# Down weights in 8 KB runs and gate_up in four sections: one MoE kernel on one core

## The chip, the cores and the metric

One Trainium2 chip; the kernel runs on one of its cores. The metric is the device time of one execution in microseconds (us). The engines are named as the profile names them: PE is TensorE (PEld its weight loads), DVE VectorE, ACT ScalarE, POOL GpSimd, SP SyncE, which issues the transfers. A "q" behind an engine's name is its sequencer, which waits, branches and issues.

## The reference

One encoder layer on 256 tokens of width 1024: three token mixers, a merge, a LayerNorm, then a mixture of experts with 32 experts of which each token takes four. The change touches the experts alone:

```python
def expert_block(args):
    xe, e = args
    h = xe @ w_gu[e] + b_gu[e]
    gate, up = h[:, :D_FF], h[:, D_FF:]
    gate = jnp.minimum(gate, SWIGLU_LIMIT)
    up = jnp.clip(up, -SWIGLU_LIMIT, SWIGLU_LIMIT)
    return ((up + 1) * (gate * jax.nn.sigmoid(SWIGLU_ALPHA * gate))) @ w_dn[e] + b_dn[e]
...
x = _layernorm(DN_ALPHA * x + ffn, ln2_g[l], ln2_b[l])
```

Each expert has a gate_up matrix of 1024 x 2048 and a down matrix of 1024 x 1024 in float32, 12 MB together. An expert's output rows are weighted by the token's gate and added to the token's row.

## The kernel before

The mixers take the first 390 us. Behind them a loop runs over the 32 experts.

**Weights.** An expert's weights are twelve tiles of 128 x 2048 float32 (1 MB): u = 0 to 7 are gate_up, u = 8 to 11 are down. `load` (L743 to L753) issues one transfer per tile on SP, in this order, into a ring of 19 slots; the transfer that takes a slot over waits until PE has done with the tile in it. The first 19 tiles are loaded during the mixers, in halves, by `do_pre`. In `wgu_v` a partition's row of a gate_up tile is one run of 8 KB in HBM. In `wdn_v` a down tile holds 256 rows of the matrix: partition p gets row p and row 128 + p of it, two runs of 4 KB.

**Tokens.** An expert's count of tokens is known only at run time. `size` is 0 for up to 32 tokens, 1 for 33 to 64, 2 for more. `expert` loads it into the engines' registers (L1198) and chooses by `tc.If`: `up_many` and the block under `both > 0` work on 64 tokens, `up_four` and the block under `both != 1` on 32. So an expert runs "four" alone, "many" alone, or both. More than 96 (`TOP`) go through the loop `heavy` (L1341), which stands in front of the last expert under an If of its own, "overflow" (L1419); with these inputs it isn't run.

**One expert on PE.** PE's order is the order of the code (`pe_order`). Gate_up runs in two sections of four tiles, `for k0 in (0, KT // 2)` (L1250): `up_many` under one If (L1251), `up_four` under the next (L1253). A bias matmul opens each accumulation (L1233 for many, L1243 for four), L1237 and L1247 are the products. Between the sections stand

- `flush(prev)`: the previous expert's rows `yh` and `yl` (a high and a low part) are scattered by matmuls with `sc` (L1172) into PSUM tiles `pos`, two for tokens 0 to 127 (c = 0), two for tokens 128 to 255 (c = 1), and DVE adds them to the sum `acc` (L1176). `pos` has two buffers, so c = 1 waits for the adds of c = 0;
- `aux`: one matmul with `rankT` (L1258) and 24 of a single column (L1119), from which slots and gates are read.

Then DVE and ACT make the gated product `uv` (tokens on partitions, 256 columns), PE turns it by two transposes per tile (L1280 for many, L1303 for four), each of 128 neighbouring columns, ACT copies the result to `hT`, and the down products follow (L1287, L1318). `weigh` makes `yh` and `yl`, which the next expert's flush takes up. In front of the overflow loop the last flush ran by itself, since that loop used the same `sc`, `yh` and `yl`.

The other engines' order is set by the framework's scheduler.

Of the kernel before, what the change touches and what calls it, by code (L numbers as in the profile page):

```python
# [10 lines left out]
F32R = mybir.dt.float32r  # L11
# [170 lines left out]
def tile_trunk(ctx, tc, xT_d, xn_d, wf_d, vec_d, row_d, rw_d, cst_d, cst2_d, rope_d, ln1_d, ln2_d,  # L182
# [539 lines left out]
    wdn_v = wdn_d.rearrange("e (h u k p) n -> e u h p k n", h=2, u=2, p=P)  # L722
# [9 lines left out]
    def do_pre(n):  # L732
        e, u = divmod(n, 12)
        assert n == nload[0]
        t = ring_tile(f"{e}_{u}")
        if u < 8:
            extra.extend([lambda n=n: nc.sync.dma_start(t[:, n:n + 1024], wgu_v[e, u][:, n:n + 1024]) for n in (0, 1024)])
        else:
            t = t.rearrange("p (k n) -> p k n", k=2)
            extra.extend([lambda k=k: nc.sync.dma_start(t[:, k], wdn_v[e, (u - 8) // 2, u % 2][:, k]) for k in range(2)])  # L740
        pre[(e, u)] = t

    def load(e, u, n=None, eng=nc.sync):  # L743

        if (e, u) in pre:
            return pre.pop((e, u))
        t = ring_tile(f"{e}_{u}", n)
        if u < 8:
            eng.dma_start(t, wgu_v[e, u])
        else:  # L750
            t = t.rearrange("p (k n) -> p k n", k=2)
            eng.dma_start(t, wdn_v[e, (u - 8) // 2, u % 2])
        return t  # L753
# [383 lines left out]

    def turned(uv, name, pT=None):
        if pT is None:
            pT = sm(f"pT{name}", [P, 2, P])  # L1140
        for j in range(2):
            T.transpose(pT[:, j], uv[:, j * P:(j + 1) * P], C("ident"))
        hT = ex.tile([P, 2, P], F32, tag="hT", name=f"hT{name}", bufs=4)
        A.activation(hT, pT, AF.Copy, scale=0.5)
        return hT
# [49 lines left out]
    def expert(e, oh, xg, bl, wt, prev, cur, fill):  # L1195
# [34 lines left out]
        def up_many(k0):  # L1230
# [3 lines left out]
            for k in range(k0, k0 + KT // 2):  # L1234
# [5 lines left out]
        def up_four(k0):  # L1240
# [4 lines left out]
            for k in range(k0, k0 + KT // 2):  # L1245
# [4 lines left out]
        for k0 in (0, KT // 2):  # L1250
# [4 lines left out]
            if k0 == 0:  # L1255
                flush(prev)
# [18 lines left out]
        with tc.If(both > 0):  # L1275
            hint(e)
            T.matmul(pY[0], bl, bdn_t, start=True, stop=False)
            for q in range(2):
                for j in range(2):
                    T.transpose(pTL[:, q, j], uv[q][2][:, j * P:(j + 1) * P], C("ident"))  # L1280
# [16 lines left out]
        with tc.If(both != 1):  # L1297
# [4 lines left out]
            for j in range(2):  # L1302
                T.transpose(pTS[:, j], uv[2][2][:, j * P:(j + 1) * P], C("ident"))  # L1303
# [85 lines left out]
    for e in range(NE):  # L1389
# [24 lines left out]
        if e == NE - 1:  # L1414

            flush(prev)
            prev = None
            free = [nload[0] + i for i in range(4)]
            with tc.If(count(NE, ALL) > TOP, label="overflow"):  # L1419
                for x in range(NE):  # L1420
                    with tc.If(count(x, ALL) > TOP):
                        for part in range(2):
                            heavy(x, part, [load(x, u, free[u % 4], PO) for u in range(12)], (f"{x}x", *parked))
# [158 lines left out]
```

## Time and profile before

| what | value |
|---|---|
| time, median of 3 runs | 1393.12 us (1392.45 to 1394.43) |
| the profiled execution | 1393.42 us |
| its span, first to last instruction | 1391.6 us |
| PE busy | 1176.0 us (85%) |
| DVE busy | 560.1 us (40%) |
| ACT busy | 332.4 us (24%) |
| read from HBM | 453.27 MB, 326 GB/s over the span |

The profile page divides the span into 40 slices and prints for each the busy share in tenths; "DMA" is the mean share of the core's 16 DMA engines, and a share may exceed 1.00 a little because packets overlap. The view of stretches gives, for each stretch, every engine's busy time with the count of its instructions, PE's granted clock (1.00 is 2.4 GHz, 0.50 is 1.2 GHz), the DMA share and the rate. The order of time gives start, duration, engine, line, operation, tiles written and read, shapes and count of merged instructions, and in brackets the engine's idle time before them with what ended it.

### The profile page before, as it was taken

To read this page: it belongs to the slowest core of one execution; us is meant where nothing else is said; L and a number is where in the kernel's file an instruction comes from. 1 tells how busy PE (TensorE), PEld (TensorE's weight loads), DVE (VectorE), ACT (ScalarE), POOL (GpSimd) and SP (SyncE) were. 2 spreads that over 40 slices of the span, in tenths; PEclk is the share of its full clock that TensorE was granted. 3 is DMA by queue.
4 is the path that set the end of the run, shared out by engine and by line. 5 is a ranking of instruction groups with operands and counts; after the bars stand their busy time and mean duration, and the time that the engine had idled before them with its cause. 6 is when DMAs were issued, how large, how long until landed. Compare 5 with 4: busy or idle time off the path is not lost. (4 is left out here: it accounts for less than half of the span.)

```text
span 1391.6 us, 21452 instructions
## 1 busy us (share of the span) xinstructions
PE 1176.0 (85%) x8019; PEld 618.2 (44%) x8019; DVE 560.1 (40%) x1206; ACT 332.4 (24%) x688; POOL 171.3 (12%) x92
## 2 busy tenths in 40 slices
PE   7999899989968988887888789898888888877875
PEld 7887789889713332332232233342322333222222
DVE  2668797857742232323222323313332322222214
ACT  5656575544421110001100101101011101000001
POOL 3432234457120000000000000000000000000000
PEclk9999899999879998999998988989989999987897
DMA  6434444567859888999999999997999999999991
GB/s 224 123 114 145 137 146 172 169 210 258 344 209 416 344 340 346 415 415 416 414 414 416 415 415 417 416 416 297 384 414 414 415 417 416 415 416 415 414 395 43
DMA packets 89497, 456.44 MB, mean 328 GB/s; under 512 B 8304, under 2 KB 8704, under 8 KB 58496
## 3 DMA queue, kind: packets, MB, share of 16 engines
q1 hardware_dynamic: 89344, 454.35, 82.5%
q8 instruction: 102, 1.67, 0.5%
q14 instruction: 51, 0.42, 0.1%
HBM read 453.27 MB, written 1.05 MB: 326 GB/s over the span
## 5 line engine op out<-in xcount | busy, mean ns | idle before, releaser
L1247 PE MATMUL pGS<-ew,xsm 128*32 128x512 f32 x1408 | 192.3, 684 | 23.1 <-DMA ew<-in_wgu_dram 11.4
L1237 PE MATMUL pGL<-ew,xg 128*64 128x512 f32 x832 | 201.5, 639 | 1.9 <-DMA ew<-in_wgu_dram 1.7
L1176 DVE TENSOR_TENSOR xn<-xn,pos 128x512 f32<-128x512 f32 x124 | 79.9, 684 | 219.0 <-PE pos L1172 216.5
L247 POOL TENSOR_TENSOR wl<-raw,wh 128x1024 fp32r<-128x1024 f32 x56 | 137.0, 2452 | 161.9 <-ACT wh L246 153.9
L1109 ACT ACTIVATE sg<-gv 128x256 f32<-128x256 f32 x48 | 20.0, 417 | 453.5 <-DVE gv L1108 452.7
L1470 POOL TENSOR_TENSOR xn<-xn,lb 128x256 f32<-128x256 f32 x4 | 2.8, 730 | 988.1 <-DVE xn L1458 988.1
L1165 DVE SCALAR_TENSOR_TENSOR yl<-pY,gsl,yh 128x512 fp32r<-128x512 f32 x35 | 26.3, 751 | 236.8 <-ACTq L1224 91.9
L1237 PEld LDWEIGHTS pGL<-ew,xg 128*64 128x64 f32 x832 | 65.5, 147 | 121.4 <-issue 112.0
L1247 PEld LDWEIGHTS pGS<-ew,xsm 128*32 128x32 f32 x1408 | 54.4, 122 | 138.8 <-issue 107.9
L1318 PE MATMUL pY<-ew,hT 128*32 128x512 f32 x704 | 90.7, 659 | 22.9 <-ACT hT L1304 21.5
L246 ACT CAST wh<-raw 128x1024 fp32r<-128x1024 f32 (+1 forms) x89 | 91.1, 1028 | 57.1 <-DMA raw<-in_wf_dram 19.9
L1287 PE MATMUL pY<-ew,hT 128*64 128x512 f32 x416 | 102.4, 650 | 0.0
L1172 PE MATMUL pos<-yh,sc 64*128 64x512 f32 x124 | 47.9, 515 | 32.0 <-DVE xn L1176 23.9
L1164 ACT ACTIVATE yh<-pY,gsl 128x512 fp32r<-128x512 f32 x35 | 24.0, 687 | 192.9 <-PE pY L1287 88.7
L247 DVE TENSOR_TENSOR wl<-raw,wh 128x1024 fp32r<-128x1024 f32 (+1 forms) x33 | 43.7, 1328 | 44.5 <-ACT wh L246 44.4
L1287 PEld LDWEIGHTS pY<-ew,hT 128*64 128x64 f32 x416 | 31.2, 149 | 62.5 <-issue 61.4
L1318 PEld LDWEIGHTS pY<-ew,hT 128*32 128x32 f32 x704 | 21.8, 119 | 77.3 <-issue 44.1
L1172 PEld LDWEIGHTS pos<-yh,sc 64*128 64x128 f32 x124 | 18.1, 190 | 83.6 <-DVE xn L1176 50.5
L1243 PE MATMUL pGS<-bgu_t,bl 128*32 128x512 f32 x176 | 25.4, 643 | 35.3 <-DVEq L1224 10.8
L1108 DVE TENSOR_SCALAR gv<-pGS 128x256 f32<-128x256 f32 x22 | 9.3, 425 | 101.2 <-PE pGS L1247 101.2
L1210 ACT COPY xsm<-xg 128x256 f32<-128x256 f32 x32 | 12.9, 402 | 141.7 <-PE pGS L1247 131.4
L1108 DVE TENSOR_SCALAR gv<-pGL 128x256 f32<-128x256 f32 x26 | 11.0, 425 | 82.9 <-PE pGL L1237 81.8
(453 smaller groups left out, 2181.1 us busy)
## 6 DMA issues: line engine op xcount, KB each, us to landing
ew<-in_wgu_dram SPq DMA_DIRECT2D x241, 1024.0 KB, 19.9
ew<-in_wdn_dram SPq DMA_DIRECT2D x124, 1024.0 KB, 20.1
raw<-in_wf_dram SPq DMA_DIRECT2D x87, 512.0 KB, 3.7
ew<-in_wgu_dram SPq DMA_DIRECT2D x30, 512.0 KB, 6.4
ew<-in_wdn_dram SPq DMA_DIRECT2D x8, 512.0 KB, 5.0
xraw<-in_xT_dram SPq DMA_DIRECT2D x4, 256.0 KB, 5.7
xn<-in_xn_dram SPq DMA_DIRECT2D x2, 512.0 KB, 5.1
lnt<-in_ln_dram SPq DMA_DIRECT2D x2, 512.0 KB, 10.7
```

The lines of the kernel that those rows point to most:

```text
L246: A.copy(h[:, b], raw[:, b])
L247: (PO if u in LOW_POOL else V).tensor_sub(l[:, b], raw[:, b], h[:, b].bitcast(F32))
L1108: V.tensor_scalar_min(gv, ps[:, 0:256], LIMIT)
L1164: A.activation(yh, pY, AF.Copy, scale=gsl)
L1165: V.scalar_tensor_tensor(yl, pY, gsl, yh.bitcast(F32), op0=ALU.mult, op1=ALU.subtract)
L1172: T.matmul(pos[n], sc[r, c * P:(c + 1) * P], y[r], start=(start and i == 0), stop=(i == 1))
L1176: V.tensor_add(dst, dst, po)
L1237: T.matmul(pL[q][h * 64:(h + 1) * 64].rearrange("p (g n) -> p g n", g=2), xg[:, k, s_], quarter(wt[k], h, q), start=False, stop=(k == KT - 1))
L1243: T.matmul(grp(pS, g), bl[:, g * TINY:(g + 1) * TINY].bitcast(F32), bgu_t[:, q * 512:(q + 1) * 512].bitcast(F32), start=True, stop=False)
L1247: T.matmul(grp(pS, g).rearrange("p (g n) -> p g n", g=2), xs_[:, k], quarter(wt[k], h, q), start=False, stop=(k == KT - 1))
L1287: T.matmul(pY[0][n * 64:(n + 1) * 64], hT[b][:, j, h * CAP:(h + 1) * CAP], wt[KT + 2 * b + h][:, j, n * 512:(n + 1) * 512], start=False, s ...
L1318: T.matmul(grp(pY, 2 * n + j), hT[:, j, g * TINY:(g + 1) * TINY], w[:, j, n * 512:(n + 1) * 512], start=(j == 1 and (b, h) == (0, 0)), sto ...
```

## The change

Four things change.

1. The down tile's view: partition p gets rows 2p and 2p + 1 of the tile's 256, one run of 8 KB. `load` and `do_pre` share one description of a tile's rows for it (`rows_of`, `shaped`). The product's rows must follow: the transposes now take every second column of `uv` (`alternate`), so that `hT[:, j]` holds rows 2p + j.
2. Gate_up runs in four sections of two tiles, each with its two Ifs.
3. `flush` is cut: c = 0 behind the first section, c = 1 behind the second, `aux` behind the third.
4. The loop over more than 96 tokens has rows of its own (`rest`, in buffers that are free then), and the flush in front of it is gone: the last expert flushes its predecessor like all others.

```diff
-    wdn_v = wdn_d.rearrange("e (h u k p) n -> e u h p k n", h=2, u=2, p=P)
+    wdn_v = wdn_d.rearrange("e (h u p k) n -> e u h p (k n)", h=2, u=2, p=P)
...
+    def rows_of(e, u):
+
+        return wgu_v[e, u] if u < 8 else wdn_v[e, (u - 8) // 2, u % 2]
+
+    def shaped(t, u):
+        return t if u < 8 else t.rearrange("p (k n) -> p k n", k=2)
...
+        eng.dma_start(t, rows_of(e, u))
+        return shaped(t, u)
...
+    def alternate(uv, j):
+
+        return uv.rearrange("t (p j) -> t j p", j=2)[:, j]
...
-            T.transpose(pT[:, j], uv[:, j * P:(j + 1) * P], C("ident"))
+            T.transpose(pT[:, j], alternate(uv, j), C("ident"))
...
-            for k in range(k0, k0 + KT // 2):
+            for k in (k0, k0 + 1):
...
-        for k0 in (0, KT // 2):
+        for k0 in range(0, KT, 2):
             with tc.If(pe > 0):
                 up_many(k0)
             with tc.If(pe != 1):
                 up_four(k0)
-            if k0 == 0:
-                flush(prev)
+            if k0 <= 2:
+                flush(prev, (k0 // 2,))
+            elif k0 == 4:
                 aux = bank(5, f"aux{e}", [P, S + 2])
...
-            flush(prev)
-            prev = None
+            rest = (mo.tile([P, S], F32R, tag="ohp", name="sch", bufs=2),
+                    *[t[:, i] for t in (mo.tile([P, 2, 512], F32R, tag="xg", name="yx", bufs=2),) for i in range(2)])
...
-                            heavy(x, part, [load(x, u, free[u % 4], PO) for u in range(12)], (f"{x}x", *parked))
+                            heavy(x, part, [load(x, u, free[u % 4], PO) for u in range(12)], (f"{x}x", *rest))
```

PE before, in expert 1, from the end of the first section of four tiles to `aux` (`pGS` is the PSUM tile of "four", `ew_1_3` the expert's fourth weight tile, `pos` the scattered rows):

```order
L1247 MATMUL pGS_4848<-ew_1_3_4084,xsm_4802 32x512 x4
L1253 UNCONDITIONAL_BRANCH x2
L1172 MATMUL pos_4889<-yh,sc 128x512
L1172 MATMUL pos_4890<-yh,sc 128x512
L1172 MATMUL pos_4889<-yl,sc 128x512
L1172 MATMUL pos_4890<-yl,sc 128x512
L1172 MATMUL pos_4897<-yh,sc 128x512
L1172 MATMUL pos_4898<-yh,sc 128x512
L1172 MATMUL pos_4897<-yl,sc 128x512
L1172 MATMUL pos_4898<-yl,sc 128x512
L1258 MATMUL aux_4905<-rankT,idr 128x256
```

PE now, at the same place: from the first half of the flush into the second section (`pGL` is the PSUM pair of "many"; lines have moved by two).

```order
L1174 MATMUL pos_4877<-yh,sc 128x512
L1174 MATMUL pos_4878<-yh,sc 128x512
L1174 MATMUL pos_4877<-yl,sc 128x512
L1174 MATMUL pos_4878<-yl,sc 128x512
L1253 COMPARE_AND_BRANCH
L1239 MATMUL pGL_4850<-ew_1_2_4083,xg_4389 64x512 x2
L1239 MATMUL pGL_4851<-ew_1_2_4083,xg_4389 64x512 x2
L1239 MATMUL pGL_4850<-ew_1_3_4084,xg_4389 64x512 x2
L1239 MATMUL pGL_4851<-ew_1_3_4084,xg_4389 64x512 x2
L1253 UNCONDITIONAL_BRANCH x2
L1255 COMPARE_AND_BRANCH
L1249 MATMUL pGS_4852<-ew_1_2_4083,xsm_4806 32x512 x4
```

The eight scatter matmuls stood in one piece; now two tiles' products and two branches stand between the first four and the second four.

PE before, ahead of the last expert (`cnt` holds the counts; L1419 is the branch over the overflow loop):

```order
L1224 UNCONDITIONAL_BRANCH x2
L1172 MATMUL pos_14253<-yh,sc 128x512
L1172 MATMUL pos_14254<-yh,sc 128x512
L1172 MATMUL pos_14253<-yl,sc 128x512
L1172 MATMUL pos_14254<-yl,sc 128x512
L1172 MATMUL pos_14261<-yh,sc 128x512
L1172 MATMUL pos_14261<-yl,sc 128x512
L1172 MATMUL pos_14262<-yh,sc 128x512
L1172 MATMUL pos_14262<-yl,sc 128x512
L1384 TENSOR_LOAD cnt
L1419 COMPARE_AND_BRANCH
```

PE now, at the same place (the second pair of rows is the loop's own start):

```order
L1226 UNCONDITIONAL_BRANCH x2
L1387 TENSOR_LOAD cnt
L1422 COMPARE_AND_BRANCH
L1387 TENSOR_LOAD cnt
L1424 COMPARE_AND_BRANCH
```

The eight scatter matmuls have moved behind the branch, into the last expert's first two sections.

## Rows read from the trace of the kernel before

**Rows 1.** The page: DMA share by slice, then gate_up transfers, us to landing.

```profile
DMA  6434444567859888999999999997999999999991
...
ew<-in_wgu_dram SPq DMA_DIRECT2D x241, 1024.0 KB, 19.9
```

**Rows 2.** Stretches: length, busy us (instructions) by engine, clock, DMA share, GB/s.

```profile
391.00:528.00 137.00, 117.99 (x732) 42.37 (x732) 42.32 (x97) 17.10 (x40) 5.75 (x3) 0.89 0.85 338
533.00:809.00 276.00, 231.47 (x1502) 84.76 (x1494) 78.84 (x191) 32.24 (x73) 0.00 (x0) 0.94 1.02 415
820.00:997.00 177.00, 157.56 (x937) 62.25 (x931) 48.73 (x117) 22.30 (x51) 0.00 (x0) 0.91 0.96 389
1002.00:1309.00 307.00, 247.01 (x1651) 85.77 (x1645) 84.61 (x201) 34.26 (x77) 0.00 (x0) 0.89 1.02 415
```

**Rows 3.** Order of time, SP: transfers issued in bursts when slots come free.

```profile
527.91 2.87 SPq L749 DMA_DIRECT2D ew<-in_wgu_dram  x4
...
996.89 4.33 SPq L749 DMA_DIRECT2D ew<-in_wgu_dram  x5
```

**Rows 4.** Stretches that hold gate_up tiles alone (two), then down tiles (two).

```profile
585.50:601.00 15.50, 13.87 (x84) 6.76 (x86) 6.99 (x17) 2.48 (x6) 0.00 (x0) 1.00 1.01 419
...
1116.10:1131.60 15.50, 13.12 (x73) 4.83 (x71) 3.82 (x8) 0.69 (x1) 0.00 (x0) 0.86 1.01 418
605.00:612.40 7.40, 5.32 (x26) 1.66 (x24) 0.98 (x2) 0.69 (x1) 0.00 (x0) 1.00 1.03 409
...
1135.60:1142.40 6.80, 6.59 (x31) 3.02 (x27) 3.38 (x9) 1.72 (x4) 0.00 (x0) 1.00 1.03 409
```

**Rows 5.** Order of time, PE: an expert of "four", first section to second.

```profile
668.55 3.64 PE L1247 MATMUL pGS<-ew,xsm 128*32 128x512 f32 x32
672.12 0.50 PE L1172 MATMUL pos<-yh,sc 64*128 64x512 f32 x2
...
673.63 1.09 PE L1172 MATMUL pos<-yh,sc 64*128 64x512 f32 x2 [0.78 <-DVE xn L1176]
...
674.89 0.38 PE L1258 MATMUL aux<-rankT,idr 128*128 128x256 f32 x1
...
676.34 5.34 PE L1247 MATMUL pGS<-ew,xsm 128*32 128x512 f32 x32 [0.51 <-PEq L1251]
```

**Rows 6.** PE's waits: who waited for whom, us in total, times, longest us.

```profile
PE pos L1172 <- DVE xn L1176: 23.9, 31, 0.9
...
PE pGS L1247 <- DMA ew<-in_wgu_dram: 11.4, 12, 2.2
...
PE pGS L1247 <- PEq L1251: 8.7, 18, 0.5
...
PE pGS L1243 <- PEq L1251: 6.5, 3, 2.8
...
PE pos L1172 <- PEq L1253: 2.8, 9, 0.3
```

**Rows 7.** Order of time, PE: second sections of "many", experts 2, 10 and 30.

```profile
462.23 8.41 PE L1237 MATMUL pGL<-ew,xg 128*64 128x512 f32 x32
...
702.27 7.09 PE L1237 MATMUL pGL<-ew,xg 128*64 128x512 f32 x32
...
1314.81 8.78 PE L1237 MATMUL pGL<-ew,xg 128*64 128x512 f32 x32
```

**Rows 8.** Two stretches of expert 30: its flush and aux, then what follows.

```profile
1311.50:1314.90 3.40, 2.56 (x35) 1.32 (x33) 2.40 (x4) 0.00 (x0) 0.00 (x0) 0.99 1.00 405
1314.90:1318.30 3.40, 3.40 (x10) 1.18 (x12) 0.24 (x2) 0.00 (x0) 0.00 (x0) 0.50 1.01 412
```

**Rows 9.** Order of time, PE: the last flush, and the last expert's first matmul.

```profile
1336.48 0.50 PE L1172 MATMUL pos<-yh,sc 64*128 64x512 f32 x2 [2.55 <-DVEq L1297]
...
1342.34 1.19 PE L1233 MATMUL pGL<-bgu_t,bl 128*128 128x512 f32 x2 [2.51 <-PEq L1419]
```

**Rows 10.** Line L1303: weight loads of its transposes, min/median/max ns.

```profile
L1303 PEld LDWEIGHTS pTS<-cst,uv x44: 137/140/227, 412.2 to 1295.3; 128*128 128x128 f32 x44
```

More of the change, by code (lines that the diff above doesn't have):

```diff
@@ L734, in do_pre @@
         assert n == nload[0]
[L735 to L741, printed above, removed]
+        t, src = ring_tile(f"{e}_{u}"), rows_of(e, u)
+        extra.extend([lambda a=a: nc.sync.dma_start(t[:, a:a + 1024], src[:, a:a + 1024]) for a in (0, 1024)])
+        pre[(e, u)] = shaped(t, u)
+    def rows_of(e, u):
+        return wgu_v[e, u] if u < 8 else wdn_v[e, (u - 8) // 2, u % 2]
+    def shaped(t, u):
+        return t if u < 8 else t.rearrange("p (k n) -> p k n", k=2)
     def load(e, u, n=None, eng=nc.sync):
@@ L747, in load @@
         t = ring_tile(f"{e}_{u}", n)
[L748 to L753, printed above, removed]
+        eng.dma_start(t, rows_of(e, u))
+        return shaped(t, u)
     nx, m2s, ys, dts, gths, att, mx, late, szs = [0], [], [], [], {}, {}, [], {}, []
@@ L1244, in up_four @@
                              bgu_t[:, q * 512:(q + 1) * 512].bitcast(F32), start=True, stop=False)
-            for k in range(k0, k0 + KT // 2):
+            for k in (k0, k0 + 1):
                 for g, (h, q) in enumerate(QUARTERS):
@@ L1279, in expert @@
                 for j in range(2):
-                    T.transpose(pTL[:, q, j], uv[q][2][:, j * P:(j + 1) * P], C("ident"))
+                    T.transpose(pTL[:, q, j], alternate(uv[q][2], j), C("ident"))
                 A.activation(hT[q], pTL[:, q], AF.Copy, scale=0.5)
@@ L1302, in expert @@
             for j in range(2):
-                T.transpose(pTS[:, j], uv[2][2][:, j * P:(j + 1) * P], C("ident"))
+                T.transpose(pTS[:, j], alternate(uv[2][2], j), C("ident"))
             A.activation(hT[2], pTS, AF.Copy, scale=0.5)
```

## Prediction

> **What bounds the kernel now.** I read the slices of the page first, then four stretches of the expert stage, then the order of time on TensorE (PE) and on SyncE (SP), then PE's waits. The reader is to see in the slices [rows 1] that from the thirteenth of the 40 on, at 417 us, the DMA engines are nearly always full, with a few dips. The stretches [rows 2] tell the dips apart. From 533 to 809 us and from 1002 to 1309 us the DMA share is 1.02: weights arrive as fast as they can. From 391 to 528 it is 0.85, from 820 to 997 it is 0.96: there transfers were held back because the ring of 19 slots was full, and PE sets the pace. The two moments at which the hold ended for good are the issues at 527.91 and 996.89 us [rows 3]; each follows the end of the down products of an expert of the "many" form. PE's idle time for weights is only 11.4 us in 12 waits in its largest group [rows 6]. So the two resources are close to balance, and the path to the end is a chain of five links: PE (391 to 528), DMA (533 to about 815), PE (820 to 997), DMA (997 to 1309), PE (1309 to the end). A saving counts only in the link where its resource stands on the path.
>
> PE's work depends on the token count: an expert runs the form "four" (at most 32 tokens), "many" (33 to 64), or both (over 64). Which bias matmul opens an expert (L1243 or L1233) tells it in the order of time. Experts 0 to 3 are four, four, both, many; 15 to 18 are both, four, both, many; 30 and 31 are many. In all there are 19 four, 10 many, 3 both.
>
> **The change, part by part.**
>
> *Down tiles with 8 KB runs.* A transfer of 1,048,576 bytes takes 2.506 us at the 418.5 GB/s of two windows that hold gate_up tiles (8 KB runs), and 2.564 us at the 409 GB/s of two that hold down tiles (two 4 KB runs per partition) [rows 4]. After the change both have the same shape in HBM and in SBUF, so I price a down tile like a gate_up tile: 0.058 us less, with 0.04 to 0.08 kept for the range, since rates are whole GB/s and the windows differ by one or two. An expert takes 8 x 2.506 + 4 x 2.564 = 30.3 us of transfer. The second link, 276 us, is 9.1 experts, 36 down tiles: -2.1 us. The fourth, 307 us, is 10.1 experts, 40 down tiles: -2.35 us. In the other links the price is nothing, because PE's time hides it.
>
> *Flush in two parts.* Before, the eight scatter matmuls of the previous expert ran in one go after four tiles, and the second four waited for VectorE's adds to free PSUM: 0.78 us in an expert of four [rows 5], 23.9 us over 31 experts, so 0.77 each [rows 6]. After the change two tiles' products lie between the halves: at full clock 3.64/2 = 1.8 us in "four" [rows 5], 3.5 us in "many", longer than two adds. I take the 0.77 us as gone. What is late next is only the branch behind each flush, priced now.
>
> *Two more sections.* An expert now has four sections, each with the two Ifs of PE. Skipping the "many" arm ahead of a "four" section left PE idle 8.7/18 = 0.48 us each time; skipping the "four" arm behind a "many" section 2.8/9 = 0.31 us [rows 6]. Two more of them cost +0.97 us in "four" and +0.62 us in "many"; in "both" no arm is skipped. Per expert, with the 0.77 us, that is +0.20 (four), -0.15 (many), -0.77 (both). The other engines pass the two extra Ifs in one or two branch instructions each; none of them issues what PE waits for there, and SP runs about eight transfers ahead, so I cost these at nothing. Their bound is one transfer's hold at a join, which a queue of 19.9 us from issue to landing [rows 1] covers.
>
> *Release of slots.* A "many" expert frees gate_up slots only where the skipped arm closes, four at a time; now two at a time. Both moments that end a hold for good [rows 3] hang on down tiles, which are freed as before. So nothing is gained from this on the path.
>
> *The clock.* In the expert of [rows 5] the second half takes 5.34 us where the first took 3.64. In expert 30 the clock went from 0.99 in the stretch that holds the flush and the small matmuls of L1258 and L1119 to 0.50 in the next one [rows 8]: 2.4 to 1.2 GHz. In the links where PE counts, the slow second halves behind a flush are in experts 2, 15, 17 and 30, 8.41 to 8.79 us (first and last in [rows 7]) against 7.09 at full clock: 1.3 + 1.7 + 1.7 + 1.7 = 6.4 us. The change puts two tiles' products after each half of the flush and before the small matmuls, so that this run of thin work is cut into three. I take the 6.4 us as regained; none of it is the other end.
>
> *Transposes read every second column.* The weight load of a transpose takes 140 ns on contiguous columns [rows 10]; no strided load is in the trace. Four loads per "many", two per "four". If each doubled, the ten experts in PE's links (three four, four many, three both) would lose 3 x 0.28 + 4 x 0.56 + 3 x 0.84 = 5.6 us, half of that if the second load of a pair hides under the first matmul. Below nothing is excluded: the same elements are read. I take 0, the row's own value, and keep 2.8 for the range.
>
> *The last expert.* Before, expert 31 began after a flush at 1336.48 that ran until 1339.83, then 2.51 us for the branch over the overflow loop [rows 9]. Now that flush lies inside: 3.35 us out; 2.0 us of matmuls (2.77 less 0.77 [rows 5]) and two skips of 0.31 in: -0.75 us. That the 2.55 and 2.51 us of waiting around it merge could save up to 2 us more; I leave it out. No instruction of that loop stands in the trace, so its own tiles cost nothing.
>
> **The sum.** Link 1: +0.97 (expert 0 has no flush) + 0.20 - 0.77 - 0.15 - 1.3 clock = -1.05. Link 2: -2.1. Link 3: -0.77 + 0.20 - 0.77 - 0.15 - 3.4 clock = -4.9. Link 4: -2.35. Link 5: -0.15 - 1.7 - 0.75 = -2.6. Together -13.0 us. The profiled execution took 1393.42 us, its span 1391.6; the median of the runs is 1393.12, 0.3 us lower. 1393.4 - 13.0 = 1380.4, so I say 1380. PE must keep up in the DMA's links for this; the 11.4 us that it waits for weights [rows 6] are the room.
>
> **Rivals.**
>
> *The clock falls as before* (1387 us). Each half of the flush now is followed by an idle 0.3 to 0.5 us, and thin stretches could move instead of vanish. For it: experts also lose the clock around the down phase, which is not touched. Against: the fall follows the flush and the small matmuls together in the rows. Without the 6.4 us, -6.6.
>
> *The down tiles land no faster* (1385 us). The change does not do what it says if the 2.3% between the two rates comes from something other than run length, such as the place of the weights in HBM. Then the 4.45 us of links 2 and 4 are gone: -8.6. For it: only four windows were set side by side. Against: it holds in both links. The Trainium skill, DMA: Bandwidth & Descriptors, section "Why small descriptors are slow (HBM only)", says that merging descriptors is only worth it at 256 B or less, since the overhead is some cycles per packet; by it 4 KB and 8 KB runs cost the same and this rival's time comes out. The trace so far disagrees, 409 against 418.5 GB/s [rows 4].
>
> *The added skips are dear* (about 1407 us, slower). There are 19 x 2 + 10 x 2 = 58 of them. After a "many" expert PE once waited up to 2.8 us, 6.5 us in three cases [rows 6], for a chain of three or four skips and register loads. If the price is x each, PE's work grows by 58x - 23.9 us; the 11.4 us of waits for weights and the 3.4 us of the last flush absorb some. With the clock as before it turns slower from x = 0.67 us; at 0.9 us it is 28.3 - 14.8 = +13.5. Against: the very skips that are doubled took 0.31 and 0.48 us in 27 cases, none above 0.5. The Trainium skill, Runtime: NRT & Kernel Launch, section "Instruction fetch mechanics", says that a taken branch whose target is not in the pages at hand stalls until they are fetched; by it every skip that leaves its page is dear, and this rival's time comes out. The trace agrees for none of the doubled skips, whose longest is 0.5 us.
>
> **How the numbers follow.** Forecast 0.60, clock as before 0.17, down tiles no faster 0.10, dear skips 0.08, and 0.05 for a mixture near no change. Low end: -13.0, another 1.6 us if a down tile saves 0.08 and a fourth less per skip, about 1.4 us, and the 2 us of the last expert: 1375. High end: no clock (+6.4), 0.04 per tile (+1.4), strided loads (+2.8): -2.4, so 1391. A measurement of this kernel can tell about 0.2%, 2.8 us, from no change. Faster by more: 0.60 + 0.17 + 0.10 less a little for their upper edges, 0.85; within: 0.07; slower: 0.08.
>
> **What would show it.** In the changed profile: windows of down tiles at 418 instead of 409 GB/s; the scatter matmuls without the 0.77 us wait; 0.48 and 0.31 us twice more per expert before sections; second halves behind the flush at 7.09 and 3.64 us at full clock; transposes' loads at 140 ns; expert 31 starting some 13 us earlier than 1342.34. The prediction is wrong if skips rise above 0.67 us, if PE's waits in links 2 and 4 vanish while its own work grew, or if the clock falls elsewhere as often.

## The result, and the profile after

| | before | after |
|---|---|---|
| median of the runs beside each other | 1393.78 us (4 runs) | 1380.60 us (4 runs) |
| ratio, 95% interval | | 0.9912 [0.9891, 0.9933] |
| the same kernel, a second time | 1395.16 us (9 runs) | 1381.83 us (5 runs), 0.9898 [0.9854, 0.9942] |
| first profiled execution | 1393.42 us | 1384.71 us |
| second profiled execution | | 1376.46 us |

The changed kernel is some 13 us faster. Its first profile is the longest of its first four runs, and its second is among the shortest; so both are used, and a difference that only one of them shows is not called an effect.

The chain of five links is the frame in which I compare. A link ends where the down products of expert 3, 14, 18, 29 and 31 end. The next fence has those five stretches of before. Columns: start and end, length, busy us (instructions) of each engine, granted clock, DMA share, GB/s.

```profile
391.10:527.20 136.10, 117.97 (x732) 42.37 (x732) 42.23 (x96) 16.31 (x38) 5.66 (x3) 0.89 0.85 340
527.20:831.10 303.90, 251.54 (x1635) 91.41 (x1633) 85.71 (x206) 34.72 (x78) 0.00 (x0) 0.93 1.01 412
831.10:996.20 165.10, 147.94 (x886) 59.00 (x883) 45.86 (x110) 19.82 (x46) 0.00 (x0) 0.92 0.96 387
996.20:1300.70 304.50, 243.53 (x1648) 85.15 (x1647) 84.61 (x201) 34.26 (x77) 0.00 (x0) 0.89 1.02 414
1300.70:1371.80 71.10, 57.93 (x276) 20.30 (x272) 13.85 (x31) 4.87 (x11) 0.00 (x0) 0.90 0.79 323
```

The same view of the changed kernel, second profile:

```profile
391.30:525.40 134.10, 115.33 (x732) 41.52 (x732) 42.31 (x96) 16.33 (x38) 5.69 (x3) 0.92 0.85 346
525.40:826.60 301.20, 241.53 (x1635) 84.03 (x1633) 86.93 (x206) 34.71 (x78) 0.00 (x0) 0.97 1.01 416
826.60:982.90 156.30, 141.33 (x884) 54.65 (x883) 46.17 (x110) 19.82 (x46) 0.00 (x0) 0.96 1.00 411
982.90:1284.20 301.30, 231.45 (x1649) 75.73 (x1647) 85.56 (x201) 34.26 (x77) 0.00 (x0) 0.94 1.01 416
1284.20:1355.00 70.80, 56.69 (x272) 18.65 (x272) 13.86 (x31) 4.90 (x12) 0.00 (x0) 0.93 0.79 328
```

Links 2 and 4 have a full DMA share in both kernels and lose 2.7 and 3.2 us. In link 3 the clock rises from 0.92 to 0.96, and it loses 8.8 us, half of the 17.1 us by which the five links of this profile are shorter. Link 5 hardly moves. In the first profile of the changed kernel the five links took 137.9, 301.8, 159.1, 301.2 and 70.7 us: links 2, 4 and 5 as here, links 1 and 3 longer, at 0.88 and 0.94.

What answers [rows 5], the order of time on TensorE (PE) in the same expert 9, first profile of after; columns are start, length, instruction, and in brackets the idle time ahead of it and what ended that:

```profile
664.23 1.93 PE L1249 MATMUL pGS<-ew,xsm 128*32 128x512 f32 x16
666.09 0.50 PE L1174 MATMUL pos<-yh,sc 64*128 64x512 f32 x2
666.42 0.40 PE L1174 MATMUL pos<-yl,sc 64*128 64x512 f32 x2
667.28 1.92 PE L1249 MATMUL pGS<-ew,xsm 128*32 128x512 f32 x16 [0.46 <-PEq L1253]
669.13 0.50 PE L1174 MATMUL pos<-yh,sc 64*128 64x512 f32 x2
669.47 0.40 PE L1174 MATMUL pos<-yl,sc 64*128 64x512 f32 x2
670.33 1.92 PE L1249 MATMUL pGS<-ew,xsm 128*32 128x512 f32 x16 [0.46 <-PEq L1253]
672.18 0.38 PE L1261 MATMUL aux<-rankT,idr 128*128 128x256 f32 x1
...
673.59 1.92 PE L1249 MATMUL pGS<-ew,xsm 128*32 128x512 f32 x16 [0.46 <-PEq L1253]
```

The wait of 0.78 us for VectorE's adds is gone, 0.46 us stands three times ahead of a section, and each section has the length that 16 products have at full clock. From the first product to the end of the last section it is 11.28 us, where before it was 13.13.

What answers [rows 6], PE's waits (total, times, longest):

```profile
PE pGS L1249 <- DMA ew<-in_wgu_dram: 26.9, 33, 1.4
PE pGS L1249 <- PEq L1253: 20.2, 41, 0.8
...
PE pos L1174 <- PEq L1255: 4.7, 20, 0.3
```

No row of scatter products waiting for VectorE is left. The wait for gate_up tiles has more than doubled (11.4 to 26.9 us): the time that PE won in links 2 and 4 turned into waiting there.

What answers [rows 4], two stretches with gate_up tiles alone and two with down tiles alone (second and fourth):

```profile
558.00:573.60 15.60, 12.06 (x115) 4.57 (x119) 7.04 (x18) 2.71 (x7) 0.00 (x0) 1.00 1.02 418
577.60:584.10 6.50, 6.19 (x31) 1.82 (x26) 1.28 (x2) 0.00 (x0) 0.00 (x0) 1.00 1.01 417
1201.20:1216.60 15.40, 11.82 (x76) 2.81 (x68) 3.55 (x6) 0.69 (x1) 0.00 (x0) 0.81 1.02 420
1220.60:1227.20 6.60, 4.27 (x34) 1.74 (x30) 3.55 (x9) 2.71 (x7) 0.00 (x0) 1.00 1.02 420
```

Down tiles went from 409 to the rate of gate_up tiles. The page counts 73472 packets on their queue where it counted 89344 before: 128 fewer for each of the 124 down tiles, one packet per partition in place of two.

What answers [rows 10], the weight loads of the strided transposes (min/median/max ns):

```profile
L1306 PEld LDWEIGHTS pTS<-cst,uv x44: 194/206/219, 415.2 to 1285.7; 128*128 128x128 f32 x44
```

They did not stay at 140 ns, and they did not double.

### The profile page after: what moved, and what is told of

Its sections match the earlier page's. It is cut to its first block, busy times and chain, and to the rows that moved or that the text cites. A ratio compares the mean times of both kernels' runs of the same rounds, so it can differ in the third digit from the quotient of the medians.

```text
span 1382.9 us, 21751 instructions
## 1 busy us (share of the span) xinstructions
PE 1153.9 (83%) x8019; PEld 599.3 (43%) x8019; DVE 561.3 (41%) x1206; ACT 332.8 (24%) x688; POOL 171.2 (12%) x92
## 3 DMA queue, kind: packets, MB, share of 16 engines
q1 hardware_dynamic: 73472, 454.35, 82.3%
HBM read 453.27 MB, written 1.05 MB: 329 GB/s over the span
## 5 line engine op out<-in xcount | busy, mean ns | idle before, releaser
L1249 PE MATMUL pGS<-ew,xsm 128*32 128x512 f32 x1408 | 189.4, 643 | 50.7 <-DMA ew<-in_wgu_dram 26.9
L1249 PEld LDWEIGHTS pGS<-ew,xsm 128*32 128x32 f32 x1408 | 44.9, 114 | 156.3 <-issue 101.7
L1321 PE MATMUL pY<-ew,hT 128*32 128x512 f32 x704 | 87.0, 629 | 29.7 <-ACT hT L1307 20.9
L1239 PEld LDWEIGHTS pGL<-ew,xg 128*64 128x64 f32 x832 | 57.9, 141 | 115.7 <-issue 95.1
L1174 PEld LDWEIGHTS pos<-yh,sc 64*128 64x128 f32 x124 | 12.4, 184 | 58.5 <-issue 58.5
L1303 PE MATMUL pY<-bdn_t,bl 128*32 128x512 f32 x88 | 24.2, 623 | 14.2 <-PEq L1294 14.2
L1174 PE MATMUL pos<-yh,sc 64*128 64x512 f32 x124 | 31.4, 495 | 4.7 <-PEq L1255 4.7
L417 DVE SCALAR_TENSOR_TENSOR xacc<-xp,vec,xacc 128x256 f32<-128x256 f32 x48 | 32.5, 676 | 4.0 <-ACT xacc L415 2.8
## 6 DMA issues: line engine op xcount, KB each, us to landing
lnt<-in_ln_dram SPq DMA_DIRECT2D x2, 512.0 KB, 10.6
```

The source lines that it names most:

```text
L417: V.scalar_tensor_tensor(acc, xp[:, j:j + S], W("cw5", t * 5 + j), acc, op0=ALU.mult, op1=ALU.add)
L1174: T.matmul(pos[n], sc[r, c * P:(c + 1) * P], y[r], start=(start and i == 0), stop=(i == 1))
L1239: T.matmul(pL[q][h * 64:(h + 1) * 64].rearrange("p (g n) -> p g n", g=2), xg[:, k, s_], quarter(wt[k], h, q), start=False, stop=(k == KT - 1))
L1249: T.matmul(grp(pS, g).rearrange("p (g n) -> p g n", g=2), xs_[:, k], quarter(wt[k], h, q), start=False, stop=(k == KT - 1))
L1303: T.matmul(grp(pY[1], 2 * n), bl[:, n * CAP:n * CAP + TINY].bitcast(F32), bdn_t.bitcast(F32), start=True, stop=False)
L1321: T.matmul(grp(pY, 2 * n + j), hT[:, j, g * TINY:(g + 1) * TINY], w[:, j, n * 512:(n + 1) * 512], start=(j == 1 and (b, h) == (0, 0)), sto ...
```

## The experiments

Beside the link times I use the microseconds that PE spent at half clock (1.2 GHz granted instead of 2.4) in links 1, 3 and 5, counted from the clock record. The mean clock of a row gives about the same: link 3 of before, 2 x 0.08 x 165.1 = 26 us. One profile of each kernel:

| kernel | links 1 to 5, us | at half clock in links 1, 3, 5 | ratio of times [95%] |
|---|---|---|---|
| before | 136.1, 303.9, 165.1, 304.5, 71.1 | 29.5, 27.3, 13.7 | 1 |
| after, first profile | 137.9, 301.8, 159.1, 301.2, 70.7 | 33.1, 20.5, 10.2 | 0.9912 [0.9891, 0.9933] |
| after, second profile | 134.1, 301.2, 156.3, 301.2, 70.7 | 22.5, 13.7, 10.2 | 0.9898 [0.9854, 0.9942] |
| down_runs | 138.7, 301.5, 163.0, 301.6, 70.2 | 34.0, 23.9, 10.2 | 0.9958 [0.9935, 0.9980] |
| four_sections | 134.7, 304.0, 155.3, 304.8, 67.9 | 26.5, 13.7, 6.8 | 0.9898 [0.9870, 0.9925] |
| last_flush | 139.2, 304.1, 169.7, 304.9, 78.4 | 34.7, 37.5, 20.5 | 1.0049 [1.0027, 1.0070] |
| whole_flush | 142.9, 316.8, 173.2, 301.3, 77.0 | 32.9, 37.5, 17.1 | 1.0172 [1.0124, 1.0219] |
| eight_sections | 140.2, 313.4, 166.2, 301.6, 75.4 | 18.4, 17.1, 13.7 | 1.0145 [1.0099, 1.0190] |
| sections_runs | 131.5, 301.4, 156.0, 301.3, 68.3 | 17.8, 13.7, 6.8 | 0.9895 [0.9853, 0.9937] |
| sections_runs_again | 134.8, 301.8, 159.0, 301.1, 70.3 | 26.6, 20.5, 10.2 | 0.9896 [0.9867, 0.9926] |
| plain_columns | 134.8, 301.8, 158.9, 301.3, 70.6 | 26.7, 20.5, 10.2 | 0.9881 [0.9841, 0.9922] |
| three_sections | 134.8, 302.1, 155.4, 301.1, 71.3 | 30.5, 17.1, 17.1 | 0.9838 [0.9812, 0.9865] |
| three_plain | 130.2, 301.8, 155.1, 301.1, 71.3 | 22.0, 17.1, 17.1 | 0.9842 [0.9810, 0.9874] |
| two_halves | 140.5, 305.2, 157.9, 304.8, 65.2 | 43.1, 20.5, 10.2 | 0.9920 [0.9890, 0.9949] |

### One part alone: the runs, the sections, the last flush

**down_runs.** To the kernel before:

```diff
-    wdn_v = wdn_d.rearrange("e (h u k p) n -> e u h p k n", h=2, u=2, p=P)
+    wdn_v = wdn_d.rearrange("e (h u p k) n -> e u h p (k n)", h=2, u=2, p=P)
...
-                    T.transpose(pTL[:, q, j], uv[q][2][:, j * P:(j + 1) * P], C("ident"))
+                    T.transpose(pTL[:, q, j], alternate(uv[q][2], j), C("ident"))
```

> The kernel before with only the 8 KB runs of the down weights and the transposes of every second column; two sections, whole flush and last flush as before. Theory: the gain is 0.058 us a down tile and only where the weights set the pace (36 tiles in the second link, 40 in the fourth), so 0.9968 of before, -4.5 us; the strided weight loads, which took 194 to 206 ns in the trace of after where they took 140, can take back up to 0.25 us in each of the twelve or so experts in which TensorE sets the end, so at worst -1.5 us. Down windows near 418 GB/s, gate_up windows at 419. Rival (the runs are no faster, or the tiles only shift the wait): 1.000, and the down windows stay at 409.

Measured: 0.9958, and links 2 and 4 fell by 2.4 and 2.9 us where 2.1 and 2.35 were priced. Nothing else of the kernel is needed for that. The cross-check is the next kernel, which has everything of the four sections but 4 KB runs, and whose links 2 and 4 stayed at 304.0 and 304.8 (last_flush, also with 4 KB runs: 304.1 and 304.9). So the term of the down tiles is shown from both sides.

**four_sections.** To the kernel before:

```diff
-            for k in range(k0, k0 + KT // 2):
+            for k in (k0, k0 + 1):
...
-        for k0 in (0, KT // 2):
+        for k0 in range(0, KT, 2):
...
-            if k0 == 0:
-                flush(prev)
+            if k0 <= 2:
+                flush(prev, (k0 // 2,))
+            elif k0 == 4:
```

> The kernel before with only the four sections of two tiles and the flush in two halves with the thin work behind the third; 4 KB runs, plain transposes and the standalone last flush as before. Theory: what TensorE sets gets shorter, the first, third and fifth link (-1.0, -4.9 and -2 us), and the two links that the weights set do not move, so -8 us, 0.9943 of before; the wait for the adds of 0.77 us is gone and 0.49 us twice more stands behind the skipped section. Rival 1 (the clock falls as before, the sections only take the wait out): -1.6 us, 0.9989, with as many half-speed windows as before. Rival 3 (the skips are dear): 1.002 or more. If the layout alone carried the gain, 1.000.

Measured: 0.9898, that is -14.2 us where -8 was expected. Link 3 alone gave -9.8, and half of its 27.3 us at half clock went. Rival 1 is out.

**last_flush.** To the kernel before:

```diff
-            flush(prev)
-            prev = None
+            rest = (mo.tile([P, S], F32R, tag="ohp", name="sch", bufs=2),
+                    *[t[:, i] for t in (mo.tile([P, 2, 512], F32R, tag="xg", name="yx", bufs=2),) for i in range(2)])
...
-                            heavy(x, part, [load(x, u, free[u % 4], PO) for u in range(12)], (f"{x}x", *parked))
+                            heavy(x, part, [load(x, u, free[u % 4], PO) for u in range(12)], (f"{x}x", *rest))
```

> The kernel before with only the flush of expert 30 moved out from ahead of the overflow test into expert 31 (own rows for the loop over 96 tokens). Theory: one flush and its wait is covered, -0.75 us, 0.9995 of before, and 6.7 us between the experts in place of 8.4. Rival: the whole flush lies on the end, -3 us, 0.998. Other rival: the time only goes from the gap into expert 31, 0 us, 1.000.

Measured: 1.0049, slower, and no theory had that. PE's order of time at the start of expert 31 in this kernel:

```profile
1348.26 1.19 PE L1240 MATMUL pGL<-bgu_t,bl 128*128 128x512 f32 x2 [8.27 <-PEq L1426]
...
1359.81 0.59 PE L1179 MATMUL pos<-yh,sc 64*128 64x512 f32 x2 [0.30 <-PEq L1260]
```

From the end of expert 30's down products to this first matmul it is 8.3 us, and before, with the whole flush in between, it was 8.4 [rows 9]. So what ends at the overflow test (L1426 here) sets this gap, and the flush had stood in it for some 0.1 us. Moved, it joined expert 31, which took 37.2 us instead of 29.5, with more of it at half clock (20.5 us in link 5 instead of 13.7). The other links' differences (link 3 +4.6) lie in experts whose instructions did not change; they go with the clock, and whether the edit has a part in them stays open.

The three ratios multiplied give 0.9905, where the changed kernel has 0.9912 and 0.9898. Within these intervals the parts add.

### Where the thin work stands

**whole_flush.** To the changed kernel:

```diff
-            if k0 <= 2:
-                flush(prev, (k0 // 2,))
-            elif k0 == 4:
+            if k0 == 0:
+                flush(prev)
```

> The changed kernel with its four sections, but the whole flush and the thin work behind the first of them. Theory: all skips stay and the wait for the adds (0.77 us in an expert of four) comes back, while the three other sections have no thin work between them: in the experts that TensorE sets (about nine) +7 us, and if it is the spreading of the thin work that kept the clock up, up to 6 us more, so 1387 to 1393 us, 0.996 to 0.999 of before. Rival (the cut into sections does it, not where the thin work stands): 1381 us, 0.991 of before.

Measured: 1.0172, far above both. Order of time on PE in its expert 20, behind the first section:

```profile
1052.26 0.50 PE L1174 MATMUL pos<-yh,sc 64*128 64x512 f32 x2
...
1053.77 1.10 PE L1174 MATMUL pos<-yh,sc 64*128 64x512 f32 x2 [0.77 <-DVE xn L1178]
...
1055.02 0.38 PE L1260 MATMUL aux<-rankT,idr 128*128 128x256 f32 x1
...
1056.49 3.20 PE L1249 MATMUL pGS<-ew,xsm 128*32 128x512 f32 x16 [0.51 <-PEq L1253]
1060.12 2.03 PE L1249 MATMUL pGS<-ew,xsm 128*32 128x512 f32 x16 [0.44 <-PEq L1253]
```

The wait for the adds is back, and the section behind the thin work takes 3.20 us where sixteen products take 1.92: the clock fell as in [rows 5] and [rows 8]. I listed, over the 19 experts of four, how long after an expert's start the clock fell. Before it fell 6.8 to 10.2 us after the start in 12 of them; here 5.8 to 8.2 us after it in 11, in both just behind flush and small matmuls. In the second profile of the changed kernel it is one, in eight_sections and three_sections none. So cutting into sections is not enough. Had sections alone done it, this kernel would have been as fast as the changed one; it is some 37 us slower, and some 24 us slower than before, whose flush it has. The slower clock is not the whole of it. In link 3, with four experts, the wait accounts for 4 x 1.3 = 5 us (its price is worked out below) and 17 to 24 us more at half clock for 8.5 to 12 us, 14 to 17 us together; link 3 took 14.1 and 16.9 us longer than in the two profiles of the changed kernel.

**two_halves.** To sections_runs (below): two sections as before, and

```diff
-            if k0 <= 2:
-                flush(prev, (k0 // 2,))
-            elif k0 == 4:
...
+            if k0 == 0:
+                flush(prev, (0,))
...
+        flush(prev, (1,))
+        aux = bank(5, f"aux{e}", [P, S + 2])
...
         fill()
```

> As sections_runs, but only two sections of four tiles as in the kernel before: the flush's first half stands behind the first, its second half and the thin work behind the last section, after VectorE's gate arithmetic in program order. No adds are waited for and there is no added skip. Theory A (the wait for the adds is what let the clock fall, the cut into sections only cost): half-clock time as in sections_runs, two skips less, -1.4 us in eight experts, of which the work moved to the end of gate_up takes back about 1 us each: -3 to -11 us, 0.982 to 0.987 of before. Theory B (the short sections are what keeps the clock up): half-clock time as in the kernel before (29.5, 27.3 and 13.7 us in links 1, 3 and 5), link 3 at 160 us or more; 0.990 to 0.995.

Measured: 0.9920, the time of theory B. But the rows don't bear out its reason: link 3 took 157.9 us, under its 160, and the kernel got a wait of its own, where both theories had none. PE's waits:

```profile
PE pgt L997 <- DVE xn L1178: 14.6, 13, 1.4
PE pgx L983 <- DVE xn L1178: 14.4, 13, 1.4
```

And PE's order of time at the end of expert 21:

```profile
1056.54 0.50 PE L1174 MATMUL pos<-yh,sc 64*128 64x512 f32 x2
...
1059.20 1.25 PE L997 MATMUL pgt<-cst,rawx 128*128 128x128 f32 x8 [1.04 <-DVE xn L1178]
1061.19 1.92 PE L1303 MATMUL pY<-bdn_t,bl 128*32 128x512 f32 x4 [0.74 <-PEq L1294]
...
1064.28 5.29 PE L1321 MATMUL pY<-ew,hT 128*32 128x512 f32 x32 [0.54 <-ACT hT L1307]
```

The adds now hold the PSUM that the gather of the next experts (L983, L997) needs. Thin work and waits follow one another there, and the down products behind them run at half clock (5.29 us instead of 3.64). The fall moved from 7 to 10 us after the start to 11.7 to 14.3, in 14 of 19 experts of four. So this run doesn't tell theory A from B; with whole_flush it tells that the clock falls behind a run of thin work and waits, wherever that stands. Which of the two it takes, the thin work or the wait in it, no run separates. Links 2 and 4 took 305 us here in spite of the 8 KB runs. The rate in them is 416 GB/s, as in the changed kernel, and 127 MB landed in each where there it was 125: the tiles kept their pace, and PE ended these links later.

### What a skip costs

**eight_sections.** To the changed kernel:

```diff
-            for k in (k0, k0 + 1):
+            for k in (k0,):
...
-        for k0 in range(0, KT, 2):
+        for k0 in range(KT):
...
-            if k0 <= 2:
+            if k0 in (1, 3):
                 flush(prev, (k0 // 2,))
-            elif k0 == 4:
+            elif k0 == 5:
```

> The changed kernel with eight sections of one tile: the flush's halves stand behind the second and the fourth, the thin work behind the sixth, so only the skipped sections double. Theory: a skip costs TensorE 0.3 us (many) to 0.5 us (four), +2 us in an expert of four and +1.2 in one of many; the ten experts that TensorE sets give +11 us, and the waits for weights in the others (38 us in all) take up nearly all of theirs (+40 us), up to +5 on top: +11 to +16 us over the changed kernel, 0.999 to 1.003 of before. Rival (skips are hidden by the weights in queue): within 3 us of the changed kernel, 0.991 to 0.993. Rival (each is dear, as 0.67 us and more, or the clock falls with them): 1.006 or more.

Measured: 1.0145, 33 us above the changed kernel's run beside it and twice the theory. It is not the clock: PE spent less time at half clock than in any other of these profiles, 80 us over all five links, where the next lowest is 101. PE's order of time in expert 5, two sections with nothing between them:

```profile
562.42 1.07 PE L1249 MATMUL pGS<-ew,xsm 128*32 128x512 f32 x8 [0.46 <-PEq L1253]
563.93 1.07 PE L1249 MATMUL pGS<-ew,xsm 128*32 128x512 f32 x8 [0.45 <-PEq L1253]
564.93 0.50 PE L1174 MATMUL pos<-yh,sc 64*128 64x512 f32 x2
```

Eight products take 1.07 us by themselves, but sixteen take 1.92, so a second eight running on would add 0.85. A cut costs the idle 0.45 us and another 0.22 us for starting again: 0.67. The experts agree: at full clock one of four takes 23.4 us instead of 20.6, 0.70 for each of four more skips, and one of many 31.7 instead of 29.0, 0.67. The idle time of a wait row is two thirds of what a skip costs, in many too, where these waits are 0.46 us each and not the 0.31 of [rows 6], which stood ahead of a flush:

```profile
PE pGL L1239 <- PEq L1255: 16.2, 35, 0.7
```

With it links 2 and 3 grew by 12 and 10 us over the second profile of the changed kernel: TensorE sets link 2 too. The DMA engines still look full there (416 GB/s over 313 us): they moved 130 MB in this link, 125 in the changed kernel, so the ring was fuller at its end while PE fell behind.

**three_sections.** To sections_runs (below); `up_many` and `up_four` take the range:

```diff
-        for k0 in range(0, KT, 2):
+        for ks in (range(0, 2), range(2, 4), range(4, 8)):
...
-            if k0 <= 2:
-                flush(prev, (k0 // 2,))
-            elif k0 == 4:
+            if ks[0] <= 2:
+                flush(prev, (ks[0] // 2,))
+            if ks[0] == 2:
```

> As sections_runs (8 KB runs, the flush of expert 30 ahead of the overflow test), but three sections of two, two and four tiles: the flush's first half behind the first, its second half and the thin work together behind the second. A section more had cost 0.7 us in an expert of either form (23.4 against 20.6 us for four more, 31.7 against 29.0). Theory: one section less gives 0.7 us back in the eight experts of one form that TensorE sets, about -5 us to sections_runs, 0.985 of before, with no more half-clock time than there (17.8, 13.7 and 6.8 us in links 1, 3 and 5). Rival (the thin work must stand alone to keep the clock up): link 3 has 25 us or more at half clock again and takes 160 us or more; 0.990 or above.

Measured: 0.9838 [0.9812, 0.9865] against 0.9896 [0.9867, 0.9926] of sections_runs_again beside it: it is the fastest of all with three_plain. An expert of four takes 20.0 us instead of 20.6. Behind the second half and the small matmuls the clock stays up:

```profile
1011.37 0.50 PE L1174 MATMUL pos<-yh,sc 64*128 64x512 f32 x2
...
1012.67 0.31 PE L1117 MATMUL aux<-Gm,ohs 128*32 128x1 f32 x16
1013.44 3.64 PE L1249 MATMUL pGS<-ew,xsm 128*32 128x512 f32 x32 [0.46 <-PEq L1253]
```

So the small matmuls need not stand alone. The expectation of no more half-clock time than in sections_runs was not met: 30.5, 17.1 and 17.1 us against 17.8, 13.7 and 6.8, though link 3 kept its length (155.4 us). Where in the chain its 9 us lie, one profile doesn't show: the five links sum to 964.7 us here, 959.5 in three_plain, and to 958.5 and 967.0 in the two profiles of sections_runs, and the half-clock time in links 1 and 5 differs from execution to execution.

### The last flush and the strided transposes within the changed kernel

**sections_runs** and **sections_runs_again.** To the changed kernel: `flush(prev)` and `prev = None` back in place of `rest`.

> The changed kernel with the flush of expert 30 back ahead of the overflow test (the 8 KB runs and the four sections stay). Theory: the gap between experts 30 and 31 is set by the test and not by the flush (8.3 to 8.4 us in the three kernels with two sections and 6.7 to 7.2 in the three with four, with the flush in it or not), so the gap stays at 6.5 to 7.5 us and expert 31 takes 1.5 to 2 us less (29 to 30 us): 1376 to 1379 us, 0.987 to 0.989 of before, the lower end if the clock in expert 31 gains too. Rival: where the flush stands is neutral, and the 1.0049 of the kernel that had it alone came from the clock in earlier experts: as the changed kernel, 0.991. Rival of the prediction: the gap grows by the flush (0.75 us), 0.9915.

> The kernel sections_runs once more, beside the two above. Theory: link 5 takes 68 us again, 2.4 less than the 70.7 of both profiles of the changed kernel (expert 31 at 29.6 us against 31.0, the gap between 30 and 31 at 6.7 to 7.5 in both), and the time is 0.989 of before; the other links differ from the changed kernel's by the clock alone. Rival: link 5 at 70 us or more, the 68.3 was chance.

Measured: 0.9895 and 0.9896, no difference to the changed kernel (0.9898 beside the first). Expert 31 took 29.6 and 30.0 us instead of 31.1 and 31.0; the gap ahead of it 7.5 and 7.4 us instead of 6.7 and 6.9. Both together are 37.1 and 37.4 us instead of 37.8 in both: moving the flush cost 0.4 to 0.7 us, where 0.75 was to be gained. Link 5 was 68.3 and 70.3, with 6.8 and 10.2 us at half clock: the second differs from the changed kernel's 70.7 by 0.4 only, so I had taken a chance of the clock for an effect. The first matmul of expert 31 in the changed kernel and in sections_runs, one fence each, tells the gap:

```profile
1332.02 1.19 PE L1235 MATMUL pGL<-bgu_t,bl 128*128 128x512 f32 x2 [6.69 <-DVEq L1422]
```

```profile
1316.09 0.50 PE L1174 MATMUL pos<-yh,sc 64*128 64x512 f32 x2 [2.55 <-DVEq L1300]
...
1320.99 1.19 PE L1235 MATMUL pGL<-bgu_t,bl 128*128 128x512 f32 x2 [1.50 <-DVEq L1422]
```

With the flush in it the gap is 7.5 us, split into 2.55, the flush with its waits, and 1.50: the flush of 3.4 us makes it 0.8 us longer.

**after_again.** The changed kernel unchanged.

> The changed kernel once more, with a second profile. Theory: the first profile (1384.7 us) was one of its slower executions; the median stays at 0.991 of before, and where the second profile is shorter than the first, the difference lies in links 1, 3 and 5, in the microseconds at half clock there (33.1, 20.5 and 10.2 in the first), while links 2 and 4 take 301 to 302 us in both. Rival: the two profiles differ in links 2 and 4 too, so that the tiles' pace itself varies.

Measured: 0.9898; links 2, 4 and 5 within 0.6 us of the first profile, links 1 and 3 shorter by 3.8 and 2.8, with 10.6 and 6.8 us less at half clock. At half clock products take twice as long (eight of four, start to start, 1.71 us against 0.86 in the kernel before), so half of these, 5.3 and 3.4 us, is what the clock can account for.

**plain_columns.** To the changed kernel (contiguous transposes, 8 KB runs kept):

```diff
-        V.tensor_scalar_min(gv, ps[:, 0:256], LIMIT)
+        V.tensor_scalar_min(halves(gv), alternate(ps[:, 0:256]), LIMIT)
...
-        V.tensor_scalar(uv, ps[:, 256:512], LIMIT, -LIMIT, op0=ALU.min, op1=ALU.max)
+        V.tensor_scalar(halves(uv), alternate(ps[:, 256:512]), LIMIT, -LIMIT, op0=ALU.min, op1=ALU.max)
```

> The changed kernel, but the order of the columns is turned round where VectorE reads the gate_up products, so that the transposes read 128 neighbouring columns as before, with the 8 KB runs kept. Theory: the weight loads of the transposes go back from 194 to 206 ns to 140, two or four in an expert, VectorE's two clips stay at 420 to 440 ns; 0.1 to 0.25 us in each of ten experts: -1 to -2.5 us to the changed kernel, 0.989 to 0.991 of before. Rival (the loads lie beside other work): 0.991. Rival (the strided read costs VectorE more than it gives): clips over 500 ns, 0.993.

**three_plain.** The same, in three_sections.

> As three_sections, with the columns' order turned round where VectorE reads the gate_up products, so that the transposes read neighbouring columns. Theory: their weight loads at 149 ns in place of 203, 0.1 to 0.2 us in eight to ten experts, -1 to -2 us to three_sections. Rival: beside other work, no difference that can be measured.

Measured: 0.9881 and 0.9842, against 0.9898 and 0.9838 of the kernels without the edit beside them: no difference that these runs can tell. The loads went back, in plain_columns:

```profile
L1308 PEld LDWEIGHTS pTS<-cst,uv x44: 137/141/224, 420.8 to 1288.2; 128*128 128x128 f32 x44
```

VectorE's clips, which now read every second column from PSUM, stayed at 415 to 425 ns. The strided load costs 65 ns, and 0.1 to 0.3 us an expert is below what the time shows.

## Why the prediction was right, point by point

The time (1380.0 forecast, 1380.6 measured) is right. That it is this close is luck: the five links gave -10.0 us in the first profile and -17.1 in the second, where -13.0 was forecast, and single links missed by up to 3.9 us. What was right is the chain of links, the term of the down tiles and the direction of the clock's; the other terms partly cancelled.

**Down tiles: right.** Forecast -2.1 and -2.35 us in links 2 and 4. The two profiles have -2.1 to -2.7 and -3.3, down_runs -2.4 and -2.9, and the layout of before with four sections none. Down tiles went from 409 to about 418 GB/s, so rival 2 falls. The rule against it, in the Trainium skill, DMA: Bandwidth & Descriptors, section "Why small descriptors are slow (HBM only)", that merging descriptors pays only up to 256 B, does not hold in this kernel: 409 GB/s with 4 KB runs, 418 with 8 KB.

**The flush wait and the skips: the sum nearly right, both terms too small.** Forecast +0.20 us net in an expert of four. In expert 9, without the clock (1.70), it is -0.15: the whole flush with its waits took 2.77 us (672.12 to 674.89 in [rows 5]) and its halves take 0.74 each, so -1.29 instead of -0.77; the cuts cost +1.14 instead of +0.97 there, and 0.67 to 0.70 each by eight_sections. At full clock throughout, the shortest experts went from 20.7 to 20.6 us (four) and from 29.4 to 29.0 (many), where +0.20 and -0.15 were forecast. The 0.77 was too small because the row of [rows 5] shows the wait ahead of its first matmul alone. The weight loads show two waits in each flush, one for each of the two PSUM tiles (order of time, in the kernel before):

```profile
672.89 1.29 DVE L1176 TENSOR_TENSOR xn<-xn,pos 128x512 f32<-128x512 f32 x2 [3.88 <-PE pos L1172]
673.63 0.18 PEld L1172 LDWEIGHTS pos<-yh,sc 64*128 64x128 f32 x1 [1.21 <-DVE xn L1176]
674.23 0.18 PEld L1172 LDWEIGHTS pos<-yh,sc 64*128 64x128 f32 x1 [0.42 <-DVE xn L1176]
```

The stretch of the second four; the clock is the third number from the right:

```profile
673.60:675.00 1.40, 1.27 (x5) 0.59 (x5) 0.80 (x2) 0.00 (x0) 0.00 (x0) 1.00 1.02 418
```

The second of the two tiles came free 0.6 us after the first, and with the clock at 1.00 the second four matmuls took 1.33 us, the first four 0.73. The reading error was the same in both terms: the idle time in a row was taken as the whole price of a stop. The turning point of rival 3 was x = 0.67 us with the clock as before, and eight_sections puts a skip there, which the prediction had named as a sign of being wrong. The changed kernel is faster all the same for two reasons. The flush's waits were worth 1.29 us and not 0.77: an estimate by the rival's own sum is 58 x 0.67 - 31 x 1.29 = -1 us of PE's work. And the clock did not stay as before. whole_flush, which has the skips and keeps the waits, shows the other side: it is slower than before.

**The clock: right in kind, its size uncertain by a factor of two.** Forecast -3.4 us in link 3, for the second halves of experts 15 and 17. The half-clock time there fell by 6.8 us in the first profile and by 13.6 in the second, which is 3.4 and 6.8 us of time. Link 3 gave -6.0 and -8.8 instead of -4.9. Its length is clear of the differences between executions: 163.0 to 169.7 us in the three kernels with two sections and the whole flush, 155.3 to 159.1 in the six profiles with four sections and the flush cut. That the clock falls behind the run of thin work and waits is borne out by whole_flush (the fall is back, as early as before) and two_halves (it moved with them); which of the two it takes stays open. In link 1 the forecast of -1.05 met +1.8 and -2.0: the clock's state there differs between executions of one kernel by more than the term. In expert 30 rival 1 came true: its gate_up is back at full clock (its last section 3.79 us), but the clock fell in the down products behind it (8.62 us instead of 7.09), so 1.7 us were priced and 0.5 came: expert 30 took 32.3 instead of 32.7 us.

```profile
1309.41 3.79 PE L1239 MATMUL pGL<-ew,xg 128*64 128x512 f32 x16
...
1316.71 8.62 PE L1290 MATMUL pY<-ew,hT 128*64 128x512 f32 x32
```

**The last expert: wrong.** The step said "3.35 us out; 2.0 us of matmuls and two skips of 0.31 in". Of the 3.35 us only 0.1 came out with two sections (8.3 us of gap without the flush, 8.4 to 8.5 with it) and 0.1 to 0.8 with more (6.7 to 6.9 without, 7.0 to 7.5 with it), because something that ends at the branch over the overflow loop, and not the flush, sets the gap; what came in was real. The term is about +0.4 to +0.7 instead of -0.75 in the changed kernel, and link 5 gave -0.4 where -2.6 was forecast. In last_flush, alone, it cost 7.3 us in link 5.

**The strided loads: the bound right, the value wrong.** I took "0, the row's own value"; they took 206 ns against 140, half of the way to the doubled load. On the time it can't be seen.

**PE must keep up in links 2 and 4: right, but with little room.** Waits for weights grew rather than vanished, and links 2 and 4 did follow the tiles' rate. eight_sections shows the edge: there link 2 grew by 12 us.

**The fastest version** of these is three_sections, 1372.4 us, with three_plain no different from it: one section less, the flush's halves still apart, and the flush of expert 30 back in the gap.

## What to carry to other kernels

A wait's idle time in a profile is a lower bound for the price of a stop: compare the start-to-start times of the same work with and without the stop (1.07 us for eight products alone, 0.85 for eight more running on) before pricing a cut. A merged row shows the wait ahead of its first instruction alone; look at what the weight loads waited for as well. Before moving work out of a gap, see what ends the gap: work that stands under another wait costs little there (0.1 to 0.8 us of 3.4 here) and more where it goes. And where the clock falls behind a run of thin work and waits, cut that run with dense work into as few pieces as keep the clock up, since every cut has its price.

## What the runs showed of the hardware

- One 8 KB run per partition in place of two of 4 KB took a 1 MB transfer from 409 to 418 GB/s.
- A weight load of 128 columns took 206 ns where it read every second fp32 column, and 140 ns on neighbouring ones; VectorE reading every second fp32 of PSUM took the same 415 to 425 ns as on neighbours.
- Less idle time is not the same as a better clock: eight_sections had 118 waits of half a microsecond ahead of "four" sections, 57.2 us, and the least time at half clock; whole_flush had 24.5 us of them and lost the clock just behind the thin work in 11 of 19 experts of four.
- The first matmul of expert 31, behind the skipped overflow loop, came 8.3 to 8.5 us after expert 30's down products with two sections. With three, four or eight it came 6.7 to 6.9 us after them without a flush in between and 7.0 to 7.5 with one. What on the engines takes this time the profile doesn't show.
